# Four groups of a feed-forward's first product begin early, differences of tokens made in it, tokens prepared two products ahead

## The chip, the cores and the metric

The kernel runs on one core of a Trainium2 chip, in one launch. The metric is the device time of one execution in microseconds; lower is better. On a core, TensorE (PE in the profile; its weight loads are PEld) multiplies matrices, VectorE (DVE), ScalarE (ACT) and GpSimd (POOL) work on tiles in SBUF and on the matmuls' results in PSUM, and SyncE (SP) issues most DMAs. Each engine runs its own instructions in the order in which they stand in its queue.

## The reference

One layer of a decoder trunk on 512 tokens of width 1024, in fp32. Three sub-layers follow each other, each between two norms: a mixing layer (a gated unit, block-sparse attention, a convolution), a cross-attention into 256 memory tokens, and a feed-forward of width 4096 with a squared ReLU. The change lies in the last one and in what leads into it:

```python
x = x + rms_norm(memory_cross_attention(h, m, w_xq[l], w_xkv[l], w_xo[l]), post_x_g[l])
h = rms_norm(x, pre_ffn_g[l])
f = jnp.square(jax.nn.relu(h @ w_ff1[l])) @ w_ff2[l]
x = x + rms_norm(f, post_ffn_g[l])
```

## The kernel before, in words

**Splitting.** Every fp32 operand is split into a high and a low part (`split`, lines 113 and 115: ScalarE rounds, VectorE subtracts), and a product takes three matmuls: low by high, high by low, high by high (lines 123 to 125 in `mm3`, line 1067 in the first product).

**Seven products.** Both matmuls of the feed-forward are cut into 2 by 2 blocks and computed with seven block products in place of eight, numbered p 1 to 7, whose operands are sums and differences of blocks. Product 1 uses blocks as they are, products 3 and 5 to 7 need sums or differences on both sides. One block product is 24 matmuls.

**The first product** (`products1`) goes over eight groups of weight columns (`GROUPS`). Four quarters of a group's weights come by SyncE's queue (`Block.load`, line 883) into a ring of `RAWS` buffers. `Block.of` splits a quarter (or a sum) for one product. `Block.sums` makes the weight sums: one addition on VectorE (line 895), a second on VectorE (line 897) or by a DMA that adds (line 868, issued from GpSimd), and a third by such a DMA. Products 1 and 2 of a group need only the first two token tiles; `EARLY` says how many groups have them ahead of the rest in the list of work. `prepare` splits weights `AHEAD` (two) products ahead. `out` takes each product out of PSUM (L1020, L1024, L1025, L1029) and squares it.

**The tokens of the first product.** `project` multiplies the attention's output by `w_xo` for the four token tiles; each tile is then added to x and normalised: squares summed on ScalarE (L189), L178 on VectorE, the power of minus a half on GpSimd (L183), L577 and L204 on VectorE. `put_ff` transposes a tile on TensorE (L935) and splits it; for tiles 2 and 3 it first makes differences and sums (L945, through `s`). Tiles 0 and 1 feed products 1 and 2; all other products need tiles 2 and 3. In the list, tile 2's `put_ff` is called before the second product and tile 3's before the fifth.

**The second product** (`products2`) goes over four chunks of 1024 hidden columns (`NM`). `tokens` makes a product's token operand: sums and differences on VectorE (L1097), then a split. Products 2, 3 and 4 stay in PSUM over all chunks. The others are added into running sums `p_sum`: in chunk 0 copied by ScalarE (L1155); in chunks 1 and 2 products 1 and 5 are copied by ScalarE (L1157) and added by a DMA from GpSimd's queue, and the rest, and all of the last chunk, are added by VectorE (L1159). `prepare` makes tokens and weights one product ahead. In the last chunk the order is 2, 1, 5, 3, 6, 7, 4, and the output's rows are put together as their products end (L1172, L1177), scaled, added and stored (`finish`).

**Order.** A scheduler places the instructions; `ahead(n)` moves an instruction forward in it, and the code's order and the free buffers decide the rest. The loads of the first groups may not be scheduled before the matmul in `ff_after`, which `put_ff` sets at tile 0.

## Time and profile before

| | us |
|---|---|
| median of 3 runs | 734.33 (733.85 to 735.06) |
| profiled execution, device time | 734.33 |
| its span | 732.5 |
| TensorE busy | 695.5 |
| VectorE busy | 530.2 |
| ScalarE busy | 433.0 |
| GpSimd busy | 132.3 |

The span runs from the first instruction to the last; the device time has 1.8 us around it. A matmul's busy time overlaps the next one's, so the distance between two starts tells its pace. An instruction's idle time is that of its engine just before it, and the name behind the arrow is what released it. Names are those of tiles: `small` holds split tokens, sums of tokens and running sums, `quarter` weights, `fhi` and `flo` their high and low parts, `fixed` the rows of x and small columns, `fq` the first product's result.

### The profile page before, as it was taken

To read this page: it belongs to the slowest core of one execution; us is meant where nothing else is said; L and a number is where in the kernel's file an instruction comes from. 1 tells how busy PE (TensorE), PEld (TensorE's weight loads), DVE (VectorE), ACT (ScalarE), POOL (GpSimd) and SP (SyncE) were. 2 spreads that over 40 slices of the span, in tenths; PEclk is the share of its full clock that TensorE was granted. 3 is DMA by queue.
4 is the path that set the end of the run, shared out by engine and by line. 5 is a ranking of instruction groups with operands and counts; after the bars stand their busy time and mean duration, and the time that the engine had idled before them with its cause. 6 is when DMAs were issued, how large, how long until landed. Compare 5 with 4: busy or idle time off the path is not lost.

```text
span 732.5 us, 10699 instructions
## 1 busy us (share of the span) xinstructions
PE 695.5 (95%) x4032; PEld 609.5 (83%) x4032; DVE 530.2 (72%) x803; ACT 433.0 (59%) x776; POOL 132.3 (18%) x143
## 2 busy tenths in 40 slices
PE   8999999997999999999998799999999999999891
PEld 6777888797887889888888799999999888787681
DVE  3479999876774892464469967655666979889797
ACT  5463478797794662353457667666677667375522
POOL 4445343243200110000012010000002021110101
PEclk9999999999999999999999899999999999999997
DMA  8460412143331430011073395567569789695603
GB/s 286 177 230 29 145 40 76 59 158 131 116 114 59 144 115 30 30 57 58 1 223 94 96 221 143 151 168 172 143 179 194 214 186 251 160 247 152 116 0 115
DMA packets 45124, 96.67 MB, mean 132 GB/s; under 512 B 4113, under 2 KB 21265, under 8 KB 45074
## 3 DMA queue, kind: packets, MB, share of 16 engines
q1 hardware_dynamic: 37344, 72.36, 28.9%
q0 software_dynamic: 6336, 23.07, 17.5%
q10 hardware_dynamic: 1394, 0.57, 0.4%
q8 instruction: 31, 0.51, 0.3%
q14 instruction: 19, 0.16, 0.1%
HBM read 70.83 MB, written 2.10 MB: 100 GB/s over the span
## 4 chain that ended last, share of the span: by engine, by line
PE 68%; DVE 17%; ACT 6%; issue 4%; POOL 3%; DMA 2%; DVEq 0%; POOLq 0%; ACTq 0%
PE ps L1067 20%; PE ps L123 15%; PE ps L125 15%; PE ps L124 15%; DVE small L115 2%; DVE flo L115 2%; DVE lo L144 2%; POOL fixed L183 2%; DVE fixed L577 1%; DMA tmp<-in_w_sT 1%; PE ps L685 1%; DVE small L1097 1%; PE ps L697 1%; DVE ps L383 1%; DVE tmp L204 1%
## 5 line engine op out<-in xcount | busy, mean ns | idle before, releaser
L1067 PE MATMUL ps<-small,fhi 128*128 128x256 f32 x896 | 163.8, 285 | 2.7 <-DVE small L115 2.0
L115 DVE TENSOR_TENSOR flo<-quarter,fhi 128x1024 fp32r<-128x1024 f32 x112 | 135.5, 1220 | 38.1 <-ACT fhi L113 34.8
L1067 PEld LDWEIGHTS ps<-small,fhi 128*128 128x128 f32 x896 | 141.2, 194 | 3.8 <-DVE small L115 2.5
L1067 PE MATMUL ps<-small,flo 128*128 128x256 f32 x448 | 127.9, 286 | 3.4 <-DVE flo L115 3.4
L113 ACT ACTIVATE fhi<-quarter 128x1024 fp32r<-128x1024 f32 x112 | 115.3, 1050 | 24.8 <-PE ps L1067 17.2
L123 PE MATMUL ps<-flo,small 128*128 128x512 f32 x224 | 88.2, 394 | 3.3 <-DVE flo L115 2.4
L1067 PEld LDWEIGHTS ps<-small,flo 128*128 128x128 f32 x448 | 86.7, 194 | 4.3 <-DVE flo L115 4.2
L123 PE MATMUL ps<-xl,hi 128*128 128x512 f32 (+1 forms) x256 | 87.3, 341 | 0.5 <-DVE xl L115 0.5
L124 PE MATMUL ps<-fhi,small 128*128 128x512 f32 x224 | 87.7, 392 | 0.0
L125 PE MATMUL ps<-fhi,small 128*128 128x512 f32 x224 | 87.7, 392 | 0.0
L125 PE MATMUL ps<-xh,lo 128*128 128x512 f32 (+1 forms) x256 | 86.3, 337 | 0.4 <-DVE lo L144 0.4
L124 PE MATMUL ps<-xh,hi 128*128 128x512 f32 (+1 forms) x256 | 86.3, 337 | 0.0
L143 ACT ACTIVATE hi<-raw 128x512 fp32r<-128x512 f32 x120 | 70.1, 625 | 14.3 <-PE ps L125 6.8
L868 POOL DMA_DIRECT2D quarter<-quarter x40 | 35.3, 888 | 237.7 <-DVE flo L115 106.5
L144 POOL TENSOR_TENSOR lo<-raw,hi 128x512 fp32r<-128x512 f32 x48 | 63.2, 1331 | 75.7 <-ACT hi L143 66.4
L183 POOL TENSOR_TENSOR fixed<-fixed 128x1 f32<-128x1 f32 x30 | 19.7, 658 | 256.3 <-DVE fixed L178 237.1
L144 DVE TENSOR_TENSOR lo<-raw,hi 128x512 fp32r<-128x512 f32 x72 | 50.6, 732 | 9.7 <-ACT hi L143 9.3
L123 PEld LDWEIGHTS ps<-xl,hi 128*128 128x128 f32 x256 | 48.6, 190 | 5.7 <-issue 0.7
L125 PEld LDWEIGHTS ps<-xh,lo 128*128 128x128 f32 x256 | 48.5, 190 | 5.8 <-DVE lo L144 0.8
L123 PEld LDWEIGHTS ps<-flo,small 128*128 128x128 f32 x224 | 42.3, 189 | 13.2 <-ACT small L113 2.8
L124 PEld LDWEIGHTS ps<-xh,hi 128*128 128x128 f32 x256 | 48.6, 190 | 4.7
L123 PE MATMUL ps<-lo,feat 128*128 128x512 f32 x128 | 50.5, 395 | 0.0
(179 smaller groups left out, 1326.9 us busy)
## 6 DMA issues: line engine op xcount, KB each, us to landing
quarter<-quarter POOLq DMA_DIRECT2D x40, 512.0 KB, 5.2
quarter<-in_w_ff SPq DMA_DIRECT2D x64, 256.0 KB, 4.3
quarter<-in_w_ff SPq DMA_DIRECT2D x32, 512.0 KB, 5.0
raw<-in_w_xk SPq DMA_DIRECT2D x8, 512.0 KB, 3.2
raw<-in_w_xv SPq DMA_DIRECT2D x8, 512.0 KB, 4.2
raw<-in_w_out SPq DMA_DIRECT2D x8, 512.0 KB, 3.5
raw<-in_w_xq SPq DMA_DIRECT2D x8, 512.0 KB, 3.9
raw<-in_w_xo SPq DMA_DIRECT2D x8, 512.0 KB, 4.4
```

The source lines that it names most:

```text
L113: nc.scalar.activation(hi, src, AF.Copy, scale=1.0 if scale is None else scale)
L115: nc.vector.tensor_tensor(out=lo, in0=src, in1=hi.bitcast(F32), op=ALU.subtract)
L123: latest[0] = nc.tensor.matmul(ps, lhsT=lh, rhs=rl, start=start, stop=False)
L124: nc.tensor.matmul(ps, lhsT=lh, rhs=rh, start=False, stop=False)
L125: nc.tensor.matmul(ps, lhsT=ll, rhs=rh, start=False, stop=stop)
L143: nc.scalar.activation(hi, raw[:, c], AF.Copy)
L144: eng.tensor_tensor(out=lo, in0=raw[:, c], in1=hi.bitcast(F32), op=ALU.subtract)
L183: nc.gpsimd.tensor_tensor(out=r, in0=v, in1=neghalf[:, 0:1], op=ALU.pow)
L204: nc.vector.scalar_tensor_tensor(out=xn, in0=src[:, c], scalar=r, in1=g[:, c], op0=ALU.mult, op1=ALU.mult)
L383: nc.vector.scalar_tensor_tensor(out=ac[:, d:], in0=y[:, 0:S - d], scalar=wdw[:, i, CONV - 1 - d:CONV - d], in1=ac[:, d:], op0=ALU.mult, o ...
L868: nc.gpsimd.dma_start(out=out, in_=in_, accum_op=ALU.add)
L1067: nc.tensor.matmul(o, lhsT=w[:, k, c], rhs=x[:, k, :], start=first_, stop=last_, skip_group_check=True)
```

## The change

- `EARLY` goes from 3 to 4 and `RAWS` from 11 to 12: eight block products stand ahead of the rest in the list.
- `ff_after` is set in `project`, once the last blocks of `w_xo` have been asked for, and the first loads and the first two `prepare` calls (now `begin1`) run at tile 0's `put_ff`, so ahead of its transposes and of the other tiles.
- Group 0's sums are asked for one product earlier, and its second sum is made by an adding DMA where it was VectorE.
- For chunk 0 of the second product (`N3S` = 1), two differences of blocks are made in the first product, one into a buffer of its own, one in place.
- In the second product tokens are prepared two products ahead (`AHEAD_X`), weights one ahead as before.
- In the last chunk products 1 and 5 are also copied by ScalarE and added by a DMA.
- The output gain `g5` is loaded in the second product, at its fifth block product.

The diff, without the parts that only rename or move code:

```diff
         wb = [wblock(w[1][b]) for b in range(4)]
+        ff_after[0] = latest[0]
...
-    EARLY = 3
-    RAWS = 11
+    EARLY = 4
+    RAWS = 12
     HALVES = 3
-    g5 = gain(a["post_ffn_g"])
...
-            ff_after[0] = latest[0]
+            begin1()
...
+    N3S = 1
+    n3s = {}
...
+    def begin1():
+        for n in range(EARLY):
+            blocks1[n] = group(n)
+            blocks1[n].load(FIRST, ff_after[0])
+        blocks1[0].load(REST, ff_after[0])
+        for at in range(AHEAD):
+            prepare1(at)
...
+        if (n, p) == (EARLY - 1, 1):
+            blocks1[0].sums(True)
...
-            if (n, p) == (EARLY - 1, 2):
-                blocks[0].sums(False)
...
+            if p == 4 and n % 2 == 1 and n // 2 < N3S:
+                m = n // 2
+                x00, x10, x11 = fq[2 * m][:, :, 0:256], fq[2 * m][:, :, 256:512], fq[2 * m + 1][:, :, 256:512]
+                n3s[m] = feats.tile([P, 4, 256], F32, tag="n3", name=nm("n3"), bufs=max(1, N3S))
+                nc.vector.tensor_tensor(out=n3s[m], in0=x00, in1=x10, op=ALU.subtract)
+                nc.vector.tensor_tensor(out=x10, in0=x10, in1=x11, op=ALU.subtract)
...
+            if m in n3s:
+                sums[m, 1], sums[m, 3] = x(1, 0), n3s[m]
...
-                th, tl = tokens(m, p)
-                ready[at] = (th, tl, [blocks[m][q].of(p) for q in range(2)])
+                ready[at] = [blocks[m][q].of(p) for q in range(2)]
...
+        def prepare_x(at):
+            if at < len(work):
+                ready_x[at] = tokens(*work[at])
...
+        ready_x = {}
+        for at in range(AHEAD_X):
+            prepare_x(at)
         prepare(0)
         for at, (m, p) in enumerate(work):
+            if at == NM:
+                g5.append(gain(a["post_ffn_g"], after=latest[0]))
+            prepare_x(at + AHEAD_X)
             prepare(at + 1)
-            th, tl, ws = ready.pop(at)
+            ws = ready.pop(at)
+            th, tl = ready_x.pop(at)
...
-            part = small([P, 2, 512], F32) if 0 < m < NM - 1 and p in (1, 5) else None
+            part = small([P, 2, 512], F32) if m and p in (1, 5) else None
```

**Behind the token work of the fourth tile.** VectorE's queue, around the end of tile 3's token splits. Before, the last token splits (`small<-xf`), the first product's result (`fq`), then the split of the weight sum of group 0 for product 5 (`quarter_818`), and others:

```order
L115 TENSOR_TENSOR small_799_4027<-xf_804_4032,small_798_4026 128x4x128
L115 TENSOR_TENSOR small_797_4025<-xf_805_4033,small_796_4024 128x4x128
L1020 TENSOR_TENSOR fq_612_3117<-ps_832_4231,tmp_828_4220 128x2x256
L115 TENSOR_TENSOR flo_824_4186<-quarter_818_4127,fhi_823_4185 128x1024
L115 TENSOR_TENSOR flo_830_4223<-quarter_776_3957,fhi_829_4222 128x1024
L895 TENSOR_TENSOR quarter_831_4227<-quarter_778_3963,quarter_825_4189 128x1024
```

After, at the same place:

```order
L115 TENSOR_TENSOR small_796_4027<-xf_804_4035,small_795_4026 128x4x128
L115 TENSOR_TENSOR small_798_4029<-xf_806_4037,small_797_4028 128x4x128
L1030 TENSOR_TENSOR fq_611_3115<-ps_830_4224,tmp_827_4218 128x2x256
L115 TENSOR_TENSOR flo_824_4186<-quarter_758_3856,fhi_823_4185 128x1024
L115 TENSOR_TENSOR flo_829_4221<-quarter_759_3859,fhi_828_4220 128x1024
L115 TENSOR_TENSOR flo_832_4253<-quarter_825_4189,fhi_831_4252 128x1024
```

The three splits are those of group 3's two weights (`quarter_758` and `quarter_759`, products 1 and 2) and of group 0's sum (`quarter_825`): the two added early products' splits stand behind the token work, and the split for product 5 behind them.

**GpSimd's queue at the hand-over.** Before, all norm factors of the tiles (L183) stand together, and the adding DMAs behind them:

```order
L144 TENSOR_TENSOR lo_2217<-raw_2210,hi_2216 128x512
L183 TENSOR_TENSOR fixed<-fixed 128x1 x16
L868 DMA quarter_3957<-quarter_3975 128x1024
L868 DMA quarter_3960<-quarter_3957 128x1024
L868 DMA quarter_3963<-quarter_4189 128x1024
```

After (L190 is the same power, L875 the adding DMA):

```order
L145 TENSOR_TENSOR lo_2217<-raw_2210,hi_2216 128x512
L190 TENSOR_TENSOR fixed<-fixed 128x1 x14
L875 DMA quarter_3862<-quarter_3865 128x1024
L190 TENSOR_TENSOR fixed<-fixed 128x1
L875 DMA quarter_3838<-quarter_3862 128x1024
L190 TENSOR_TENSOR fixed<-fixed 128x1
L875 DMA quarter_3841<-quarter_3838 128x1024
L875 DMA quarter_3844<-quarter_4256 128x1024
```

Group 0's second sum (`quarter_3862`) and third (`quarter_3838`, which reads the second) now stand ahead of the last two factors.

**VectorE's queue in the last chunk.** `small_1002` is the running sum of product 1, `small_1003` that of product 5; `flo_1228` and `flo_1230` are weight splits for product 5. Before:

```order
L115 TENSOR_TENSOR flo_1228_6890<-quarter_1222_6851,fhi_1227_6889 128x1024
L115 TENSOR_TENSOR flo_1230_6894<-quarter_1223_6855,fhi_1229_6893 128x1024
L1159 TENSOR_TENSOR small_1002_5893<-ps_1231_6897,small_1002_5893 128x512
L1159 TENSOR_TENSOR small_1002_5893<-ps_1232_6898,small_1002_5893 128x512
L1177 TENSOR_TENSOR small_1233_6925<-small_1002_5893,ps_996_5887 128x512
L1177 TENSOR_TENSOR small_1233_6925<-small_1002_5893,ps_997_5888 128x512
L570 TENSOR_TENSOR tmp_1235_6929<-small_1233_6925,gain_609_3113 128x512
L570 TENSOR_TENSOR tmp_1237_6934<-small_1233_6925,gain_609_3113 128x512
L1097 TENSOR_TENSOR small_1238_6936<-small_1224_6883,fq_616_3121 128x1024
L1159 TENSOR_TENSOR small_1003_5894<-ps_1246_6952,small_1003_5894 128x512
L1097 TENSOR_TENSOR small_1239_6938<-fq_617_3122,small_1238_6936 128x1024
L1159 TENSOR_TENSOR small_1003_5894<-ps_1247_6953,small_1003_5894 128x512
```

After, where L1206 is an output row, L577 its scaling, and L1114 a token sum:

```order
L115 TENSOR_TENSOR flo_1233_6901<-quarter_1225_6860,fhi_1232_6900 128x1024
L115 TENSOR_TENSOR flo_1245_6950<-quarter_1177_6616,fhi_1244_6949 128x1024
L115 TENSOR_TENSOR flo_1247_6954<-quarter_1178_6618,fhi_1246_6953 128x1024
L1206 TENSOR_TENSOR small_1237_6934<-small_1002_5894,ps_996_5888 128x512
L1206 TENSOR_TENSOR small_1237_6934<-small_1002_5894,ps_997_5889 128x512
L577 TENSOR_TENSOR tmp_1239_6938<-small_1237_6934,gain_1062_6112 128x512
L577 TENSOR_TENSOR tmp_1241_6943<-small_1237_6934,gain_1062_6112 128x512
L115 TENSOR_TENSOR small_1243_6946<-small_1226_6888,small_1242_6945 128x1024
L1114 TENSOR_TENSOR small_1251_6987<-fq_615_3119 128x1024
L115 TENSOR_TENSOR flo_1255_6994<-quarter_1171_6604,fhi_1254_6993 128x1024
L115 TENSOR_TENSOR flo_1257_6999<-quarter_1172_6606,fhi_1256_6998 128x1024
```

The two additions into `small_1002` are gone, as are those into `small_1003`. The splits for product 3 (`flo_1245`, `flo_1247`) stand ahead of the first output row, which reads `small_1002`; the token split for product 6 (`small_1243`) and its weight splits (`flo_1255`, `flo_1257`) stand behind it.

## Rows read from the trace of the kernel before

**Rows 1.** Part 1 of the page: busy microseconds, share of the span and instruction count of each engine.
```profile
PE 695.5 (95%) x4032; PEld 609.5 (83%) x4032; DVE 530.2 (72%) x803; ACT 433.0 (59%) x776; POOL 132.3 (18%) x143
```

**Rows 2.** Stretches of the span: microseconds from its start and length, then for each engine its busy time and its instructions, TensorE's granted clock as a share of full speed, the busy share of the DMA engines and what they moved.
```profile
409.00:412.00 3.00, 1.01 (x4) 0.59 (x4) 3.00 (x6) 2.15 (x4) 0.00 (x0) 0.87 0.00 0
412.00:415.00 3.00, 1.32 (x6) 1.32 (x7) 3.00 (x4) 2.21 (x3) 0.00 (x0) 0.50 0.00 0
415.00:418.00 3.00, 3.00 (x16) 3.00 (x16) 3.00 (x3) 0.00 (x0) 0.00 (x0) 0.50 0.52 158
...
415.00:560.00 145.00, 145.00 (x1195) 144.63 (x1194) 95.02 (x90) 95.17 (x128) 14.94 (x17) 0.99 0.68 170
...
690.00:700.00 10.00, 7.56 (x27) 5.73 (x26) 10.00 (x11) 4.66 (x5) 0.00 (x0) 0.83 0.07 14
```

**Rows 3.** TensorE in order of time from 376 to 422 us: start, duration, engine, line, operation, tiles, count, and in brackets its idle time before, with what ended it.
```profile
380.46 1.04 PE L935 MATMUL ps<-fixed,tmp 128*128 128x128 f32 x8
...
386.21 0.50 PE L1067 MATMUL ps<-small,fhi 128*128 128x256 f32 x2 [0.62 <-ACT fhi L113]
...
399.46 0.38 PE L1067 MATMUL ps<-small,flo 128*128 128x256 f32 x1 [0.53 <-DVE flo L115]
...
410.15 1.10 PE L1067 MATMUL ps<-small,fhi 128*128 128x256 f32 x4 [1.96 <-DVE small L115]
413.68 0.58 PE L1067 MATMUL ps<-small,flo 128*128 128x256 f32 x1 [2.43 <-DVE flo L115]
...
418.22 0.40 PE L1067 MATMUL ps<-small,flo 128*128 128x256 f32 x2
```

**Rows 4.** Who waited for whom in SyncE's queue from 345 to 420 us: total, times, longest.
```profile
SPq L883 <- DVE fixed L577: 39.3, 1, 39.3
```

**Rows 5.** ScalarE in order of time, from 360 to 400 us.
```profile
372.96 0.60 ACT L189 ACTIVATE tmp<-ps 128x512 f32<-128x512 f32 x1 [1.67 <-PE ps L125]
...
385.11 2.00 ACT L113 ACTIVATE fhi<-quarter 128x1024 fp32r<-128x1024 f32 x2
```

**Rows 6.** GpSimd in order of time, from 380 to 400 us. L183 is the power of minus a half that turns a mean square into the norm's factor; L868 issues an adding DMA.
```profile
384.85 1.39 POOL L183 TENSOR_TENSOR fixed<-fixed 128x1 f32<-128x1 f32 x1 [2.92 <-DVE fixed L178]
389.09 0.55 POOL L183 TENSOR_TENSOR fixed<-fixed 128x1 f32<-128x1 f32 x1 [2.85 <-DVE fixed L178]
392.49 1.40 POOL L183 TENSOR_TENSOR fixed<-fixed 128x1 f32<-128x1 f32 x1 [2.85 <-DVE fixed L178]
397.08 1.06 POOL L868 DMA_DIRECT2D quarter<-quarter  x1 [3.19 <-DVE xf L945]
```

**Rows 7.** VectorE in order of time, from 376 to 418 us.
```profile
377.77 1.42 DVE L204 SCALAR_TENSOR_TENSOR tmp<-fixed,gain_row 128x512 f32<-128x512 f32 x2 [0.73 <-POOL fixed L183]
...
392.27 1.22 DVE L115 TENSOR_TENSOR flo<-quarter,fhi 128x1024 fp32r<-128x1024 f32 x1
393.92 1.42 DVE L204 SCALAR_TENSOR_TENSOR tmp<-fixed,gain_row 128x512 f32<-128x512 f32 x2 [0.44 <-POOL fixed L183]
395.26 1.22 DVE L897 TENSOR_TENSOR quarter<-quarter,quarter 128x1024 f32<-128x1024 f32 x1
396.39 0.69 DVE L945 TENSOR_TENSOR xf<-ps,tmp 128x512 f32<-128x512 f32 x1
...
412.42 2.35 DVE L115 TENSOR_TENSOR flo<-quarter,fhi 128x1024 fp32r<-128x1024 f32 x2
```

**Rows 8.** TensorE in order of time in the second product, from 624 to 720 us.
```profile
625.23 0.50 PE L123 MATMUL ps<-flo,small 128*128 128x512 f32 x1 [0.43 <-DVE small L1159]
...
664.03 0.50 PE L123 MATMUL ps<-flo,small 128*128 128x512 f32 x1 [0.43 <-DVE small L1159]
...
693.96 0.47 PE L123 MATMUL ps<-flo,small 128*128 128x512 f32 x1 [2.44 <-DVE flo L115]
...
695.31 0.63 PE L125 MATMUL ps<-fhi,small 128*128 128x512 f32 x1
...
716.98 0.39 PE L124 MATMUL ps<-fhi,small 128*128 128x512 f32 x1
717.21 0.39 PE L125 MATMUL ps<-fhi,small 128*128 128x512 f32 x1
```

**Rows 9.** VectorE in order of time at the end, from 676 us on.
```profile
686.13 0.69 DVE L1159 TENSOR_TENSOR small<-ps,small 128x512 f32<-128x512 f32 x1 [0.67 <-PE ps L125]
...
712.19 0.69 DVE L1159 TENSOR_TENSOR small<-ps,small 128x512 f32<-128x512 f32 x1 [0.37 <-PE ps L125]
...
726.58 2.74 DVE L577 SCALAR_TENSOR_TENSOR fixed<-tmp,fixed 128x512 f32<-128x512 f32 x4 [0.50 <-POOL fixed L183]
```

**Rows 10.** GpSimd in order of time in the second product, from 600 us on.
```profile
677.80 0.87 POOL L868 DMA_DIRECT2D quarter<-quarter  x1 [4.89 <-DVE flo L115]
678.93 0.89 POOL L868 DMA_DIRECT2D quarter<-quarter  x1 [0.27 <-issue]
...
686.79 0.87 POOL L868 DMA_DIRECT2D quarter<-quarter  x1 [2.56 <-DMA quarter<-quarter]
```

**Rows 11.** Issue to landing of adding DMAs: first the one issued at 678.93; then the minimum, median and maximum over all of them (L868); then the same over the four that add a product into its running sum.
```profile
quarter<-quarter POOLq DMA_DIRECT2D x1, 512.0 KB, 7.5
...
DMA to landing us min/median/max: 4.5/5.2/9.8
...
DMA to landing us min/median/max: 5.3/8.4/9.8
```

More of the change, by code (lines that the diff above doesn't have):

```diff
@@ L120, in trunk @@
     latest = [None]
+    ff_after = [None]
     def mm3(ps, lh, ll, rh, rl, start, stop):
@@ L168, in trunk, with not_before, gain @@
     nc.gpsimd.memset(neghalf, -0.5)
-    def gain(src, queue=nc.sync):
+    def not_before(d, other):
+        if other is not None:
+            tc.add_manual_dep(d.ins, other.ins.name, mybir.DependencyInfo(
+                mybir.DependencyClass.NoSync, mybir.DependencyReason.DATA), reason="room")
+    def gain(src, queue=nc.sync, after=None):
         g = gains.tile([P, D], F32, tag="gain", name=nm("gain"))
-        queue.dma_start(out=g, in_=bass.AP(tensor=src.tensor, offset=src.offset, ap=[[0, P], [1, D]]))
+        not_before(queue.dma_start(out=g, in_=bass.AP(tensor=src.tensor, offset=src.offset, ap=[[0, P], [1, D]])),
+                   after)
         return g
@@ L876, in __init__, with load @@
             self.raw = {}
-        def load(self, ats, not_before=None):
+        def load(self, ats, after=None):
             for at in ats:
@@ L974, in group @@
         return Block([P, 4, 256], src)
-    def products1(xs):
-        work = [(n, p) for n in range(EARLY) for p in (1, 2)]
-        for n in range(GROUPS):
-            one = [(n, p) for p in ((5, 6, 3, 7) if n < EARLY else (1, 5, 2, 6, 3, 7))]
-            work += one[:1] + ([(n - 1, 4)] if n else []) + one[1:]
-        work.append((GROUPS - 1, 4))
-        blocks = {}
-        ready = {}
+    N3S = 1
+    n3s = {}
+    work1 = [(n, p) for n in range(EARLY) for p in (1, 2)]
+    for n in range(GROUPS):
+        one = [(n, p) for p in ((5, 6, 3, 7) if n < EARLY else (1, 5, 2, 6, 3, 7))]
+        work1 += one[:1] + ([(n - 1, 4)] if n else []) + one[1:]
@@ new lines, in trunk, with prepare1 @@
+    work1.append((GROUPS - 1, 4))
+    blocks1 = {}
+    ready1 = {}
+    FIRST, REST = ((0, 0), (1, 0)), ((0, 1), (1, 1))
+    def begin1():
[5 more added lines that the diff above has]
+            prepare1(at)
+    def prepare1(at):
+        if at >= len(work1):
+            return
+        n, p = work1[at]
+        ready1[at] = blocks1[n].of(p)
+        if p == 1 and n >= EARLY:
+            blocks1[n].sums(False)
+        if (n, p) == (EARLY - 1, 1):
+            blocks1[0].sums(True)
+        if p == 6 and n + 1 < EARLY:
+            blocks1[n + 1].sums(False)
+        if p == 5 and n + 1 < GROUPS:
+            if n + 1 >= EARLY:
+                blocks1[n + 1] = group(n + 1)
+                blocks1[n + 1].load(FIRST)
+            blocks1[n + 1].load(REST)
@@ L984, in products1 @@
+    def products1(xs):
+        work, ready = work1, ready1
         banks = {}
         kept = {}
-        FIRST, REST = ((0, 0), (1, 0)), ((0, 1), (1, 1))
-        for n in range(EARLY):
-            blocks[n] = group(n)
-            blocks[n].load(FIRST, ff_after[0])
-        blocks[0].load(REST, ff_after[0])
-        def prepare(at):
-            if at >= len(work):
-                return
-            n, p = work[at]
-            ready[at] = blocks[n].of(p)
-            if p == 1 and n >= EARLY:
-                blocks[n].sums(False)
-            if (n, p) == (EARLY - 1, 2):
-                blocks[0].sums(False)
-            if p == 6 and n + 1 < EARLY:
-                blocks[n + 1].sums(False)
-            if p == 5 and n + 1 < GROUPS:
-                if n + 1 >= EARLY:
-                    blocks[n + 1] = group(n + 1)
-                    blocks[n + 1].load(FIRST)
-                blocks[n + 1].load(REST)
@@ L1045, in out @@
                     square(quarter(1, 0), two(ps))
-        for at in range(AHEAD):
-            prepare(at)
         for at, (n, p) in enumerate(work):
```

12 lines of the change are left out of this document (5 added, 7 removed).

## The prediction

> **What bounds the kernel now.** I read the busy shares first: TensorE is busy 95% of the span, so only its gaps, its clock and the tail behind its last product can be won [rows 1]. The table by stretch came next: the clock is full nearly everywhere and half in two places, both in the feed-forward; between 415 and 560 us TensorE has no gap at all, with VectorE busy 95.02 of 145 us there [rows 2]. Then TensorE in order of time: in the hand-over from the cross-attention's output projection to the first feed-forward product it has short waits (0.62 and 0.53 us among them) and two long ones, 1.96 us for a token split and 2.43 us for a weight's low part; behind the second the matmuls run at half clock until 418.2, at some 0.21 us apart in place of 0.12, which costs about 4.5 × (1 − 0.12 / 0.21) = 1.9 us [rows 2, 3]. In the second product there are two waits of 0.43 us for VectorE's additions into the running sums, and one of 2.44 us at 693.96, again followed by half clock [rows 8]. Last, the tail: after the last matmul only VectorE, GpSimd and the store work [rows 9].
>
> Three stretches can change: the hand-over, the two small waits, and the last chunk with its tail.
>
> **The hand-over.** What ends the long waits? VectorE. From 393.92 it runs without a gap: the last tile's two norm products, then one 1.22 us sum, three 1.22 us splits and 21 operations on 128x512 until the weight split at 412.42, whose first instruction lets TensorE go on at 413.68 [rows 3, 7]. The starts at 395.26 and 396.39 give a pitch of 1.13 us to a big operation; (412.42 − 395.26 − 4 × 1.13) / 21 = 0.60 to a small one.
>
> The new order has the same 21 small operations there, two splits and no sum (that one became a DMA), so 2 × 1.13 + 21 × 0.60 = 14.9 us in place of 17.2: 2.3 us less. It is not all won, for two reasons.
> - The earlier loads. Before, the first of them waits 39.3 us for the first tile's norm [rows 4]; now they start some 7 us sooner, and three weight roundings come onto ScalarE ahead of the second tile's square sum. Three take 3 × 1.0 = 3.0 us; ScalarE was idle 1.67 us there, so the square sum is 1.3 us later [rows 5]. On VectorE a weight split of 1.13 stands ahead of that tile's norm. Its norm products, ready at 379.2 (377.77 + 1.42), come at about 381.6, and the transposes that ran at 380.46 without a wait now wait [rows 3, 7]: 1.1 us for TensorE, and for the last two tiles behind it.
> - GpSimd's queue. Two of group 0's sums are DMA additions that now stand ahead of the fourth tile's two roots (L183), one ahead of each; the second waits until the first has landed. The first goes out behind the root that ran at 384.85 for 1.39, now 1.1 later, so at 387.4 (its weights have landed by then); with the 5.2 us of a middling addition [rows 11] it lands at 392.6; the second's issue takes 1.06 [rows 6], and the last root, due at 392.49 + 1.1 = 393.6, starts at 393.7 to 394.0: 0.4 us late at most.
>
> So the last norm is 1.5 us late, the chain 2.3 us shorter: the split that frees TensorE is 0.8 us earlier. TensorE has two more matmuls done by then (0.2 us). I take −1.0. The wait itself stays, for the splits of the two extra products stand behind all token operations of the fourth tile, and no other work is put into the gap; so the clock falls again. Bounds: −2.5 (no delay), and +3.3 if the first addition lands after 9.8 us, the longest in rows 11 (397.2, then 1.06: the root 4.7 us late). The row of 5.2 is nearer: the 9.8 was of a sum with another addition right ahead of it.
>
> There is one row against this. The root took 1.40 us at 392.49 beside a 1.22 us VectorE operation and 0.55 us at 389.09 without one [rows 6, 7]. The Trainium skill (SBUF — State Buffer, "SBUF: two separate sides") says that GpSimd and VectorE share a port pair under an exclusive lock, and that descriptors of a DMA issued from GpSimd starve behind VectorE. By it both new issues would be held by some 0.85 us each (1.40 − 0.55) in this dense stretch, and the gain of 1.0 falls to nothing; the row on the root agrees with the rule, while the issue at 397.08 took 1.06 beside VectorE's work, against 0.87 at 677.80. I keep the row of the issue.
>
> **The middle.** The two differences moved into the first product cost 2 × 1.13 us of VectorE where it has 50 us to spare [rows 2]: nothing. Preparing tokens two products ahead takes token work from in front of VectorE's additions into the sums, and these are what ended the two waits of 0.43 us: −0.9. The gain vector's load, moved among the weight loads, is wanted only in the last chunk: nothing. Bounds: 0 if another row holds these additions, −0.9 otherwise.
>
> **The last chunk and the tail.** Call E1 the end of its product 1 (686.1 [rows 9]); the span ends 46.4 us later. Today VectorE adds that product into its sum as soon as it ends. Now ScalarE copies it (two copies) and GpSimd adds it by a DMA that stands behind the last weight sum, issued at E1 + 0.7 [rows 10]; it is issued at about E1 + 1.7. Of two additions 1.1 us apart (677.80 and 678.93) the second landed after 7.5 us, and the four sums of this kind took 5.3 to 9.8 [rows 10, 11]. With 7.5 the sum is there at S = E1 + 9 (a little under, 8.8, as no weight loads run beside it).
>
> What waits for S? VectorE's first output row, and it stands in VectorE's queue ahead of the tokens and weight splits of product 6 (p 6), the one after product 3. Product 3's wait of 2.44 us goes, and its half clock (0.43 us a matmul from 694.5 to 697.9: some 1.7 us), since its tokens and splits now stand ahead of that row [rows 8]; it ends at E1 + 10.9 (two products of 24 matmuls, 0.227 us from start to start [rows 8]). But p 6 starts at S + 4 × 0.60 + 3 × 1.13 = S + 5.8 = E1 + 14.6, 3.7 us after TensorE is free, and at half clock for as long as before. p 6 then ends at S + 5.8 + 5.4 + 1.9, p 7 at S + 18.5. From p 7's end to the span's end is 20.35 us today (712.15, where the addition at 712.19 begins [rows 9], to 732.5). Now two sums of 2.35 us together are out of the first rows' way, one split of 1.13 comes in front of the last product's second half, which then waits some 4 us for it, at half clock; I count 19.6. Together S + 38.1 = E1 + 46.9, against E1 + 46.4: +0.5. Bounds, by the landing alone: 5.3 with an issue at E1 + 1.2 gives S = E1 + 6.5 and −1.8; 9.8 behind an issue at E1 + 1.7 gives S = E1 + 11.5 and +3.2. Four additions of 0.60 fewer on VectorE change nothing while it waits for S.
>
> The Trainium skill (DMA: Bandwidth & Descriptors, "Anatomy of one DMA — SWDGE (gpsimd) path") fits such a DMA by 2.0 us and its bytes at 436 GB/s, an estimate of 3.2 us for 512 KB; by it p 6 would not be held at all, the last chunk would gain about 5 us and the sum would be near −7. Of all additions of this trace none landed in under 4.5 us [rows 11], so the measurement decides.
>
> **Sum.** −1.0 − 0.9 + 0.5 = −1.4 us. The profiled execution took 734.33 us (span 732.5), which is also the median shown, so 732.9 us.
>
> **Rivals.**
> - The sum lands at the quick end. For it: in the last chunk no weight loads run. Against: another addition is in flight. End −1.8, total −3.7: 730.6.
> - The sum lands before p 6 wants anything, by S = E1 + 5.1: no wait, no half clock, p 7 ends at E1 + 21.8 and the span at E1 + 41.4, so −5.0 at the end: 727.4. Against it: the shortest landing, 4.5, behind the issue at E1 + 1.2 still gives E1 + 5.7. The Trainium skill's page DMA: Bandwidth & Descriptors (the section above) speaks for it.
> - The two extra products do fill the gap. For it: their weights are in early, and the rounding of both is on ScalarE in time. Against: VectorE's order. It would win 1.96 + 2.43, and the 1.9 of half clock, with the middle and the end as above: 727.6.
> - Slower: the sum of p 1 lands late and holds VectorE's queue. Place: VectorE's first output row of the last chunk. It decides from a landing of about 8.5 us (where the end costs more than the rest wins); at 9.8 the end is +3.2, and if the DMA additions ahead of the roots eat the hand-over's gain as well, −0.9 + 3.2 = +2.3: 736.6.
> - The change doesn't do what it says: the early groups stand behind the tokens, and the 0.43 us waits were held by something else, with the end neutral: 734.2.
>
> **How the numbers follow.** Chances: forecast 0.45 (its own range 731.4 to 734.4), quick landing 0.16, no hold 0.04, gap filled 0.06, late landing 0.20, no effect 0.09. Faster by over 0.2% (1.47 us, about what a measurement of this kernel can tell) is half of the forecast (0.22) with the next three: 0.48. Slower is the late landing, 0.20; the rest, 0.32, is within 0.2%. The range 729.5 to 736.6 leaves out the filled gap and the case without a hold, and the outer parts of the two landings.
>
> **What would show it.** TensorE's first long wait of the hand-over, now for a low part with four early groups: if it ends near 412.8 the first term is right; if there is no wait of over 1 us between 400 and 420, the filled gap is. A wait of GpSimd for an addition's landing ahead of the fourth tile's last root would show its queue. No waits of 0.43 us before 670. In the last chunk: VectorE idle for several microseconds before its first output row, released by an addition's landing, and TensorE idle ahead of p 6 by about 3.7 us; no such wait, and the end is better than I say. A second wait, of some 4 us, in the last product. I am wrong if the clock stays full through the hand-over, or if the time between the first and the second product, where I expect nothing, moves.

## The result, and the profile after

The changed kernel took 739.84 us (median of 6, 738.05 to 742.95) against 733.73 us before: ratio 1.0089, 95% interval 1.0062 to 1.0115. It is slower by 0.9%; the forecast was 732.9 us. The profiled execution is the quickest of the six (738.05 us, span 736.3).

Part 1 of the page after answers to [rows 1]: TensorE is as busy as before, in a longer span.

```profile
PE 697.7 (95%) x4032; PEld 610.1 (83%) x4032; DVE 527.8 (72%) x798; ACT 435.6 (59%) x780; POOL 134.7 (18%) x146
```

TensorE in order of time after, its waits from 396 us on (columns as in [rows 3]; L1075 is the first product's matmul, L124 and L126 those of the second):

```profile
400.64 0.47 PE L1075 MATMUL ps<-small,fhi 128*128 128x256 f32 x2 [2.03 <-DVE xf L948]
...
408.16 0.50 PE L1075 MATMUL ps<-small,fhi 128*128 128x256 f32 x2 [1.31 <-ACT fhi L113]
...
411.30 0.58 PE L1075 MATMUL ps<-small,flo 128*128 128x256 f32 x1 [1.69 <-DVE flo L115]
...
433.64 0.47 PE L1075 MATMUL ps<-small,fhi 128*128 128x256 f32 x2 [0.47 <-DVE fq L1030]
...
443.02 0.38 PE L1075 MATMUL ps<-small,flo 128*128 128x256 f32 x1 [0.27 <-DVE flo L115]
...
458.94 0.39 PE L1075 MATMUL ps<-small,flo 128*128 128x256 f32 x1 [1.26 <-DVE flo L115]
...
557.70 0.47 PE L124 MATMUL ps<-flo,small 128*128 128x512 f32 x1 [0.60 <-DVE flo L115]
...
628.55 0.50 PE L124 MATMUL ps<-flo,small 128*128 128x512 f32 x1 [2.41 <-DVE small L1188]
...
667.49 0.50 PE L124 MATMUL ps<-flo,small 128*128 128x512 f32 x1 [0.57 <-DVE small L1188]
...
703.15 0.80 PE L124 MATMUL ps<-flo,small 128*128 128x512 f32 x1 [2.73 <-DVE flo L115]
...
723.15 0.50 PE L124 MATMUL ps<-flo,small 128*128 128x512 f32 x1 [4.58 <-DVE flo L115]
```

Read against [rows 3] and [rows 8]: in place of the two long waits of the hand-over (1.96 and 2.43) stand 2.03, 1.31, 1.69 and one of 0.45 us at 409.11 that isn't shown. Three waits between 430 and 460 and one at the start of the second product (0.60) are new. The two waits of 0.43 in the second product have become 2.41 and 0.57. The 2.44 of [rows 8] is gone, and 2.73 and 4.58 stand in the last chunk.

To compare stretches I count from t0, the start of the first tile's transposes in the hand-over (374.13 before, 372.50 after). Executions differ by about 2 us ahead of it: the 1000th matmul starts at 200.4 before and at 198.7, 198.4 and 200.7 in three profiles of the changed kernel, long before its first new load (350 us). In both kernels the transposes start 0.24 or 0.23 us behind the start of the matmul in front of them, so t0 is the same point of the work in both. The table by stretch (columns as in [rows 2]; the number behind PE's busy time is its instructions), from t0 + 11.8 to t0 + 60 and from there to t0 + 90, of the kernel before:

```profile
385.93:434.13 48.20, 41.98 (x318) 40.32 (x319) 42.05 (x52) 32.56 (x52) 7.20 (x9) 0.93 0.52 120
434.13:464.13 30.00, 30.00 (x252) 30.00 (x251) 19.60 (x19) 19.86 (x27) 2.29 (x3) 1.00 0.71 186
```

and of the changed kernel:

```profile
384.30:432.50 48.20, 42.33 (x325) 41.12 (x325) 38.15 (x51) 30.07 (x50) 7.13 (x8) 0.93 0.44 99
432.50:462.50 30.00, 28.00 (x229) 27.42 (x228) 21.20 (x21) 17.80 (x26) 3.47 (x4) 1.00 0.79 194
```

At 0.12 us a matmul, the hand-over has won (325 − 318) × 0.12 = 0.8 us, and the 30 us behind it lose (252 − 229) × 0.12 = 2.8 us. From t0 to the end of the last chunk's product 1 (E1) it took 686.1 − 374.1 = 312.0 us before and 689.6 − 372.5 = 317.1 after; from E1 to the end of the span 46.4 and 46.7. So the whole loss lies ahead of the last chunk: −0.8, +2.8, +0.6 at the start of the second product, and 2.41 + 0.57 − 2 × 0.43 = +2.1 in it make 4.7 of the 5.1 us.

This profile is of the quickest execution, and one cost is missing from it. Here the clock stays full behind the wait of 2.41 us; in the second and third profile of the same kernel (runs `again` and `again2` below) it falls to half there (0.50 from 631 to 633 us in `again`, so 1.2 of 2.4 GHz). The first 4 us behind that wait, in this profile and in that of `again`:

```profile
628.55:632.55 4.00, 4.00 (x18) 3.31 (x19) 4.00 (x5) 0.36 (x1) 0.79 (x1) 1.00 0.76 262
```

```profile
629.49:633.49 4.00, 4.00 (x11) 3.18 (x12) 4.00 (x5) 0.36 (x1) 0.79 (x1) 0.62 0.74 262
```

The 168 matmuls of that chunk take 38.8 us before, 40.8 in this profile and 42.4 in the two others: where the clock falls, the wait costs 3.6 us and not 2.0.

What stands behind the waits? VectorE after, in order of time (columns as in [rows 7]; L901 and L899 are weight sums, L1206 an output row):

```profile
393.81 1.42 DVE L211 SCALAR_TENSOR_TENSOR tmp<-fixed,gain_row 128x512 f32<-128x512 f32 x2 [1.94 <-POOL fixed L190]
...
410.02 4.62 DVE L115 TENSOR_TENSOR flo<-quarter,fhi 128x1024 fp32r<-128x1024 f32 x4
...
440.61 1.22 DVE L901 TENSOR_TENSOR quarter<-quarter,quarter 128x1024 f32<-128x1024 f32 x1 [2.32 <-DMA quarter<-in_w_ff]
...
456.53 1.23 DVE L901 TENSOR_TENSOR quarter<-quarter,quarter 128x1024 f32<-128x1024 f32 x1 [2.53 <-DMA quarter<-in_w_ff]
...
697.20 1.29 DVE L1206 TENSOR_TENSOR small<-small,ps 128x512 f32<-128x512 f32 x2 [3.68 <-DMA small<-small]
```

The split that frees TensorE starts at 410.02 (first of four) and not at 412.42 [rows 7]. But two weight sums, at 440.61 and 456.53, wait 2.32 and 2.53 us for weights to land, and TensorE waits (0.27 and 1.26) for the split right behind each. The first of the two new differences stands between them, at 442.88. Such a wait of a sum alone is not new: before, one waited longer, and TensorE had no gap.

```profile
436.04 1.23 DVE L895 TENSOR_TENSOR quarter<-quarter,quarter 128x1024 f32<-128x1024 f32 x1 [3.43 <-DMA quarter<-in_w_ff]
```

Further on in the changed kernel, the first output row waits 3.68 us for a DMA addition. ScalarE after, with a token rounding (L113) and the copies of product 1 in the last chunk (L1186):

```profile
622.16 1.06 ACT L113 ACTIVATE small<-fq 128x1024 fp32r<-128x1024 f32 x1 [2.49 <-DMA small<-small]
...
688.22 0.60 ACT L1186 ACTIVATE small<-ps 128x512 f32<-128x512 f32 x1 [3.26 <-PE ps L126]
689.58 0.60 ACT L1186 ACTIVATE small<-ps 128x512 f32<-128x512 f32 x1 [0.76 <-PE ps L126]
```

The rounding at 622.16 waits 2.49 us for the landing of an addition into a running sum, although its operand is a block of `fq`. The addition still in flight is that of product 5's copy, issued at 616.30. Everything on VectorE behind the rounding is late, down to the addition into the sum that ends TensorE's wait of 2.41. GpSimd after (L190 the tiles' factor, L875 an adding DMA), answering to [rows 6] and [rows 10]:

```profile
385.48 1.39 POOL L190 TENSOR_TENSOR fixed<-fixed 128x1 f32<-128x1 f32 x1 [2.91 <-DVE fixed L185]
387.07 1.06 POOL L875 DMA_DIRECT2D quarter<-quarter  x1 [0.20 <-issue]
388.60 0.56 POOL L190 TENSOR_TENSOR fixed<-fixed 128x1 f32<-128x1 f32 x1 [0.47 <-DVE fixed L185]
392.29 0.89 POOL L875 DMA_DIRECT2D quarter<-quarter  x1 [3.13 <-DVE fixed L185]
392.91 0.86 POOL L190 TENSOR_TENSOR fixed<-fixed 128x1 f32<-128x1 f32 x1
...
616.30 0.88 POOL L875 DMA_DIRECT2D small<-small  x1 [8.93 <-ACT small L1186]
...
690.06 0.86 POOL L875 DMA_DIRECT2D quarter<-quarter  x1 [2.59 <-DMA quarter<-quarter]
690.67 1.16 POOL L875 DMA_DIRECT2D small<-small  x1
```

### The profile page after: what moved, and what is told of

Its sections match the earlier page's. It is cut to its first block, busy times and chain, and to the rows that moved or that the text cites. A ratio compares the mean times of both kernels' runs of the same rounds, so it can differ in the third digit from the quotient of the medians.

```text
span 736.3 us, 10717 instructions
## 1 busy us (share of the span) xinstructions
PE 697.7 (95%) x4032; PEld 610.1 (83%) x4032; DVE 527.8 (72%) x798; ACT 435.6 (59%) x780; POOL 134.7 (18%) x146
## 5 line engine op out<-in xcount | busy, mean ns | idle before, releaser
L1075 PE MATMUL ps<-small,fhi 128*128 128x256 f32 x896 | 164.1, 286 | 4.6 <-DVE xf L948 2.0
L1075 PEld LDWEIGHTS ps<-small,fhi 128*128 128x128 f32 x896 | 141.4, 194 | 5.9 <-ACT fhi L113 5.0
L113 ACT ACTIVATE fhi<-quarter 128x1024 fp32r<-128x1024 f32 x112 | 115.7, 1050 | 31.0 <-PE ps L1075 21.4
L1075 PE MATMUL ps<-small,flo 128*128 128x256 f32 x448 | 128.0, 286 | 3.2 <-DVE flo L115 3.2
L124 PE MATMUL ps<-flo,small 128*128 128x512 f32 x224 | 89.0, 397 | 10.9 <-DVE flo L115 7.9
L1075 PEld LDWEIGHTS ps<-small,flo 128*128 128x128 f32 x448 | 86.9, 194 | 4.0 <-DVE flo L115 4.0
L126 PE MATMUL ps<-fhi,small 128*128 128x512 f32 x224 | 88.4, 395 | 0.0
L124 PE MATMUL ps<-xl,hi 128*128 128x512 f32 (+1 forms) x256 | 87.3, 341 | 0.5 <-DVE xl L115 0.5
L126 PE MATMUL ps<-xh,lo 128*128 128x512 f32 (+1 forms) x256 | 86.2, 337 | 0.0
L875 POOL DMA_DIRECT2D quarter<-quarter x41 | 35.8, 873 | 244.5 <-DVE flo L115 107.1
L144 ACT ACTIVATE hi<-raw 128x512 fp32r<-128x512 f32 x120 | 70.1, 625 | 16.8 <-PE ps L126 10.0
L190 POOL TENSOR_TENSOR fixed<-fixed 128x1 f32<-128x1 f32 x30 | 20.0, 667 | 242.8 <-DVE fixed L185 223.5
L124 PEld LDWEIGHTS ps<-flo,small 128*128 128x128 f32 x224 | 42.9, 191 | 21.6 <-DVE flo L115 8.1
L124 PEld LDWEIGHTS ps<-xl,hi 128*128 128x128 f32 x256 | 48.6, 190 | 5.7 <-issue 0.7
L126 PEld LDWEIGHTS ps<-xh,lo 128*128 128x128 f32 x256 | 48.5, 190 | 5.1
L124 PE MATMUL ps<-lo,feat 128*128 128x512 f32 x128 | 50.6, 395 | 0.0
```

The source lines that it names most:

```text
L113: nc.scalar.activation(hi, src, AF.Copy, scale=1.0 if scale is None else scale)
L124: latest[0] = nc.tensor.matmul(ps, lhsT=lh, rhs=rl, start=start, stop=False)
L126: nc.tensor.matmul(ps, lhsT=ll, rhs=rh, start=False, stop=stop)
L144: nc.scalar.activation(hi, raw[:, c], AF.Copy)
L190: nc.gpsimd.tensor_tensor(out=r, in0=v, in1=neghalf[:, 0:1], op=ALU.pow)
L875: nc.gpsimd.dma_start(out=out, in_=in_, accum_op=ALU.add)
```

## The experiments

Every run is compared with the kernel before on the same chip; the ratios have 95% intervals. All start from the changed kernel.

**The base again** (`again`, unchanged).

> The changed kernel once more, as the base of this call. Expected: 736 to 741 us, 0.5 to 1.1% slower than before; TensorE's waits as in its first trace: about 2.0 us in all between 430 and 460 us, 2.4 near 628, 0.6 near 667, 2.7 near 703 and 4.6 near 723.

739.95 us, 1.007 (1.0047 to 1.0092), with 0.60, 2.07 and 1.22 between 430 and 460, and 2.38, 0.57, 2.61 and 4.57 later. The waits are the change's, not one execution's; their sizes between 430 and 460 vary with the landings: the sum that waited 2.32 us in the first profile waits 4.10 here, and TensorE's wait behind it is 2.07 in place of 0.27.

**The last chunk by VectorE** (`lastdve`).

```diff
-            part = small([P, 2, 512], F32) if m and p in (1, 5) else None
+            part = small([P, 2, 512], F32) if 0 < m < NM - 1 and p in (1, 5) else None
```

> The changed kernel with products 1 and 5 of the last chunk added by VectorE, as before. Theory (the landing of product 1's sum holds VectorE's queue for 3.68 us, and with it product 6): the wait near 703 goes, VectorE gets four additions of 0.60 back, and from the end of product 1 to the end of the span it takes 42 to 44 us in place of 46.75: 3 to 4 us faster than the changed kernel. Rival (the tail is VectorE's own work, the hold is only moved): within 0.7 us of the changed kernel.

736.53 us, 1.0034 (1.0014 to 1.0055): 3.4 us faster than the base. TensorE's long waits from 630 us on:

```profile
632.36 0.50 PE L124 MATMUL ps<-flo,small 128*128 128x512 f32 x1 [2.35 <-DVE small L1188]
...
701.00 0.50 PE L124 MATMUL ps<-flo,small 128*128 128x512 f32 x1 [0.61 <-DVE flo L115]
...
724.56 0.79 PE L124 MATMUL ps<-flo,small 128*128 128x512 f32 x1 [4.20 <-DVE flo L115]
```

The hold in front of product 6 is 0.61 where it was 2.61. From E1 to the end it took 738.1 − 695.0 = 43.1 us. So tokens two ahead are worth 46.4 − 43.1 = 3.3 us in the last chunk, and the DMA addition takes back 46.7 − 43.1 = 3.6: the change put both in, and the end stood still.

**Tokens one ahead, last chunk by VectorE** (`x1lastdve`: the edit above and `AHEAD_X = 1`).

> As the run before it, and tokens one product ahead. Theory (two products ahead is what makes the additions late): the wait of 2.41 near 628 is back to 0.4 and the 0.57 near 667 too, so the end of product 1 of the last chunk comes 2.1 us earlier; but product 3's splits stand late again and its 2.44 us wait with half clock returns, +3 to +4: in sum 1 to 2 us slower than the run before it. Rival (the wait near 628 comes from elsewhere): the 2.41 stays.

741.68 us, 1.0089 (1.0062 to 1.0116), 5 us slower than the run before it (single times of both spread over 5 to 7 us), where I expected 1 to 2. The last chunk behaved (2.43 near 701 is back, 46.3 us from E1). But the wait near 628 did not go; it became 1.60 at 617.54, 0.48 at 618.73 and 1.40 at 632.44. Two ahead is therefore not the cause by itself. VectorE in this run:

```profile
613.78 1.23 DVE L1114 TENSOR_TENSOR small<-small,fq 128x1024 f32<-128x1024 f32 x1 [3.60 <-DMA small<-small]
```

Now a token sum (L1114), not a rounding, waits 3.60 us for an addition's landing. What both share is the pool of 14 buffers called `small`: operands, token sums, the copies `part` that a DMA reads, and the running sums all turn in it.

**Three early groups** (`early3`: `EARLY = 3`, `RAWS = 11`).

> The changed kernel with three early groups and eleven weight buffers, as before. Theory (with four groups early, twelve buffers leave the later groups' loads too late): the waits of 0.47, 0.27 and 1.26 between 430 and 460 go, the gap of the hand-over grows by 0.6 to 1 us: 1 to 1.5 us faster than the changed kernel at the end of the first product. Rival (these waits come from the two differences made in the first product): they stay, and the time does not move or gets longer.

736.44 us, 1.0033 (1.0013 to 1.0053), 3.5 us faster than the base, more than expected. The same two stretches from its t0 (373.88):

```profile
385.68:433.88 48.20, 43.54 (x331) 42.56 (x331) 40.56 (x52) 32.36 (x54) 8.88 (x10) 0.93 0.61 145
433.88:463.88 30.00, 30.00 (x252) 30.00 (x251) 21.45 (x20) 20.28 (x28) 1.75 (x2) 1.00 0.66 171
```

331 and 252: no wait between 430 and 460, so the fourth group (with its twelfth buffer) is what brought those waits. The 13 matmuls more than before in the hand-over are not a gain, for here t0 itself is late. With three groups weight roundings on ScalarE and a weight split on VectorE stand ahead of the first tile's norm, and TensorE waits for that norm:

```profile
373.88 1.32 PE L938 MATMUL ps<-fixed,tmp 128*128 128x128 f32 x8 [0.80 <-DVE tmp L211]
```

These transposes start 1.18 us behind the start of the matmul in front of them (372.70), where it was 0.24 us before and 0.23 with four groups. From that matmul to the last one of the first product it took 186.2 us before (373.89 to 560.12), 189.2 in the changed kernel and 186.1 with three groups (372.70 to 558.75). The early loads, with group 0's DMA sum, win nothing on balance; without the fourth group they lose nothing either.

**One more small buffer** (`early3_s15`: three groups, `bufs=15` for `small`).

> Three early groups and eleven weight buffers, and 15 buffers for the tiles called small in place of 14. Theory (the ring of these buffers: a token split made two products ahead takes the buffer of a product that a DMA is still adding, ScalarE waits 2.47 us for its landing at 619.67, and VectorE's additions behind it come late): the 2.40 us wait of TensorE near 626 falls to 0.5 or less, 2 us faster than with three early groups alone (736.4). Rival (VectorE's order alone: token splits stand ahead of the additions): the wait stays at 2 us or more.

736.79 us, 1.0036 (1.0022 to 1.0051); 2.43 near 628 and ScalarE's 2.50 for the landing are as they were, where I expected them to go. One more buffer shifts who takes which, and the rounding still waits for the addition of product 5's copy (issued at 616.05), so the run does not decide between the buffer and VectorE's order.

**Both undone** (`early3_lastdve`).

> Three early groups and eleven buffers, and the last chunk's products 1 and 5 added by VectorE. If the two costs are separate, as I take it, their gains add: 3.5 and 3.4 off the changed kernel, so 733 us, level with before. Rival (one covers the other): 735 or more.

734.12 us, 0.9986 (0.9971 to 1.0002). The two gains add (739.95 − 3.5 − 3.4 = 733.0) to within 1.1 us.

**Only the earlier loads, group 0's DMA sum and the gain's late load** (`x1lastdve_e3n0`: three groups, one ahead, `N3S = 0`, last chunk by VectorE).

> Of the change only the earlier loads, the DMA addition for group 0's sum and the late load of the output gain: three early groups, tokens one product ahead, no differences in the first product, the last chunk by VectorE. Theory: the first product ends 1.4 us earlier than before (as with three early groups), and the second product is as before, with waits of 0.4, 0.4 and 2.4: 732.5 to 733. This also tells where the 1.60 us wait near 617 came from that tokens one ahead showed with the differences made early: theory, two token sums fewer shift the ring of small buffers, so without them it goes; rival (the gain's load or the order of weights and tokens): it stays.

734.06 us, 1.0004 (0.9990 to 1.0018), where I expected 732.5 to 733. The 1.60 near 617 is gone, with waits of 0.66, 0.86 and 2.43 against 0.43, 0.43 and 2.44 before. From t0 to the end its profile is 1.7 us shorter than before (356.7 and 358.3), but t0 is 0.95 late here too; from the matmul ahead of it to the first product's last it took 186.3 us against 186.2. So the earlier loads and group 0's DMA sum together are worth about nothing.

**Thirteen weight buffers** (`raws13n0`: four groups, `RAWS = 13`, `N3S = 0`).

> Four early groups with 13 weight buffers, and no differences in the first product (their buffer makes the room). Theory (the ring of weight buffers is what makes the loads of the next groups late): the waits between 430 and 460 us, 2.0 to 3.9 in sum, fall under 0.5, and the first product ends 1.5 to 3 us earlier than in the changed kernel. Rival (the order of the four groups on VectorE and GpSimd): they stay.

739.58 us, 1.0072 (1.0057 to 1.0087), against 1.0070 for `again`: no gain. Only one wait (0.34) is left between 430 and 460, but the hand-over had 319 matmuls in its 48 us where the base's profiles had 325 and 329. The waits behaved, the time did not. The run `n0` below differs from this one in the thirteenth buffer alone and had 0.93 us of waits there, so most of what went, went with the differences. SyncE's loads wait for buffers in every version; the longest such wait between 380 and 470 us is 29.1 us in the changed kernel, 29.2 in `n0`, 16.8 with thirteen buffers and 20.8 before.

**The copies in a buffer of their own** (`e3_ld_part`: three groups, last chunk by VectorE).

```diff
-            part = small([P, 2, 512], F32) if m and p in (1, 5) else None
+            part = feats.tile([P, 2, 512], F32, tag="part", name=nm("part"), bufs=1) if 0 < m < NM - 1 and p in (1, 5) else None
```

> Three early groups, the last chunk by VectorE, and the copies of products 1 and 5 (of chunks 1 and 2) in a buffer of their own and no longer among those called small. Theory (the tokens for the next chunk's product 1, made two products ahead, take the buffer of product 5's copy, which is free only when its addition has landed): ScalarE's wait of 2.5 us for the landing near 620 goes and TensorE's 2.4 us near 626 falls to 0.7 or less: 731.5 to 732.5, 1.5 to 2.5 us below the run with three early groups and the last chunk by VectorE (734.1). Rival (VectorE's order alone): the landing's wait goes, TensorE's stays at 1.5 or more.

731.40 us, 0.9965 (0.9949 to 0.9981): 2.7 us under the same kernel without it (734.12, measured at another time beside its own runs of the kernel before; by the means it is 2.0, give or take 1.2), and faster than both kernels of this document. ScalarE's rounding, VectorE's additions into the sum, and TensorE's waits from 600 us on:

```profile
619.14 1.06 ACT L113 ACTIVATE small<-fq 128x1024 fp32r<-128x1024 f32 x1 [2.00 <-PE ps L125]
```

```profile
623.65 0.68 DVE L1188 TENSOR_TENSOR small<-ps,small 128x512 f32<-128x512 f32 x1
624.81 0.69 DVE L1188 TENSOR_TENSOR small<-ps,small 128x512 f32<-128x512 f32 x1 [0.48 <-PE ps L126]
```

```profile
658.46 0.50 PE L124 MATMUL ps<-flo,small 128*128 128x512 f32 x1 [1.02 <-DVE flo L115]
...
692.00 0.50 PE L124 MATMUL ps<-flo,small 128*128 128x512 f32 x1 [0.61 <-DVE flo L115]
...
715.58 0.80 PE L124 MATMUL ps<-flo,small 128*128 128x512 f32 x1 [4.20 <-DVE flo L115]
```

No wait for a landing, the second addition now waits for TensorE (0.48), and the 2.4 us is gone; VectorE's queue still has a token split and two weight splits right ahead of the additions. So the buffer was the cause. That chunk takes 38.1 us here, against 42.4 in the profile of the same kernel without the own buffer, where the clock fell behind the wait.

**The same without the two differences** (`e3_ld_part_n0`: also `N3S = 0`).

> The same without the two differences made in the first product. Theory: these moved 2.4 us of VectorE's work out of the second product's first chunk, where nothing waits for it; no wait goes or comes: within 0.7 us of the run before it. Rival: without them a wait of over 0.5 us appears where the second product starts.

730.63 us, 0.9962 (0.9943 to 0.9981): no difference that shows. With three groups the two differences are worth nothing that can be measured here.

**Group 0's second sum by VectorE** (`e3_ld_part_sd`: `blocks1[0].sums(False)`).

> As the first of this call, and group 0's second sum by VectorE as before. Theory (GpSimd's second issue, which waits for the first addition to land, makes the fourth tile's last root 1.1 us late: VectorE idle 1.94 us before it in the changed kernel): the root comes 1.1 us earlier, the sum's 1.13 us of VectorE comes back behind it, so the split that frees TensorE moves by less than 0.3 us and the time stays within 0.7 us. Rival (the landing costs the hand-over more than the sum did): 1 us faster.

733.89 us, 0.9996 (0.9983 to 1.0010): 2.5 us slower than `e3_ld_part`, neither theory's. VectorE in the hand-over, in this run and then the same norm products in `e3_ld_part`:

```profile
390.88 1.22 DVE L901 TENSOR_TENSOR quarter<-quarter,quarter 128x1024 f32<-128x1024 f32 x1
392.02 0.21 DVE L185 TENSOR_SCALAR fixed<-fixed 128x1 f32<-128x1 f32 x1
...
394.49 1.42 DVE L584 SCALAR_TENSOR_TENSOR fixed<-tmp,fixed 128x512 f32<-128x512 f32 x2 [0.53 <-POOL fixed L190]
...
399.66 1.42 DVE L211 SCALAR_TENSOR_TENSOR tmp<-fixed,gain_row 128x512 f32<-128x512 f32 x2 [0.79 <-POOL fixed L190]
```

```profile
396.08 1.42 DVE L211 SCALAR_TENSOR_TENSOR tmp<-fixed,gain_row 128x512 f32<-128x512 f32 x2 [1.97 <-POOL fixed L190]
```

The sum (L901, 390.88) stands ahead of the fourth tile's first step (L185, 392.02), and that tile's norm products come at 399.66, 24.2 us behind its t0 (375.50), against 396.08 − 375.08 = 21.0 in `e3_ld_part`. Once the loads are early, the DMA addition is worth 2.5 us; it makes up for what they cost.

**Four groups in this version** (`e4_ld_part_n0`: `EARLY = 4`, `RAWS = 12`).

> The version without differences in the first product, with the copies' own buffer and the last chunk by VectorE, but with the change's four early groups and twelve weight buffers. Theory (the fourth group costs by itself, through weights that land late between 430 and 460 us): 3 to 3.5 us slower than with three groups (730.6), so 733.5 to 734.2, with waits of 2 us or more in sum between 430 and 460. Rival (the cost came from the two differences or from the other parts): 731.5 or less, no such waits.

731.48 us, 0.9966 (0.9952 to 0.9980), where I expected 733.5 or more. Waits of 0.62 and 0.53 between 430 and 460, against 2.0 to 3.9 in sum in the base's three profiles. So the rival held: the fourth group costs much less here than with the differences.

**The change without the differences** (`n0`, beside the base, `again2`).

> The changed kernel without the two differences in the first product, all else as changed. Theory A (four groups cost much only together with the differences: weight sums that land late leave VectorE no slack, and the differences take 2.4 us of it): the waits between 430 and 460 us fall to about 1.2 in sum, as in the version with the own buffer, and it is 2 to 3 us faster than the changed kernel. Theory B (four groups cost by themselves): within 1 us of the changed kernel, waits of 2 us or more.

> The changed kernel again, as the base beside it: 739 to 740.5 us.

740.27 us, 1.0083 (1.0061 to 1.0104), beside 742.16, 1.0104 (1.0082 to 1.0127). TensorE's waits between 430 and 460 without the differences:

```profile
435.04 0.48 PE L1075 MATMUL ps<-small,fhi 128*128 128x256 f32 x2 [0.47 <-DVE fq L1030]
...
444.60 0.39 PE L1075 MATMUL ps<-small,flo 128*128 128x256 f32 x1 [0.46 <-DVE flo L115]
```

0.93 in sum against 0.45 + 1.82 + 1.23 = 3.5 in `again2`. The last of the three is gone, as the second weight sum starts 14.1 us behind the first here and 15.9 us in `again2`, where a difference stands between them. The medians lie 1.9 apart, just under what theory A gave; the two intervals overlap, but of the twelve times only one of `n0` (741.77) reaches those of the base (741.71 and up). Theory A holds by the waits, and about in size.

## Why the prediction was wrong, by its own steps

Two terms failed: the zero for everything between the hand-over and the second product, and the −0.9 for the middle, which had the wrong sign. The hand-over and the last chunk came out as forecast.

- **The hand-over, −1.0: right.** The split that frees TensorE came 0.8 us earlier from t0 (37.5 against 38.3; forecast 0.8), the wait stayed and the clock fell. Its parts came out too: the last norm products 1.5 us later (21.3 against 19.8; forecast 1.5), the chain behind them 2.3 us shorter (16.2 against 18.5; forecast 2.3). One part was lucky: the last root, whose input was there at about 391.9, ran at 392.91, 0.9 us late by GpSimd's queue in place of 0.4 at most, but took 0.86 us in place of 1.40. The first loads came 20 us sooner (350.0 in place of 369.9) and not some 7; with three groups their roundings and splits therefore also hold the first tile's norm, and on balance the earlier loads are worth nothing there.
- **Behind the hand-over: the step that failed first.** I read in [rows 2] that TensorE has no gap from 415 to 560 and VectorE 50 us to spare, and priced the fourth group and the two differences there at nothing. An average over 145 us doesn't show how little time the splits had to spare behind a sum that waits for its weights. With four groups such sums wait 2.32 and 2.53 us (rows above), a difference stands between them, and TensorE lost 2.8 us. Without the fourth group this loss is gone (252 matmuls). Without the differences most of the waits are gone (0.93 us in place of 3.5), but not most of the time: from the matmul ahead of t0 to the first product's last it took 186.1 to 186.8 us in the six profiles with three groups and the DMA sum, 188.0 to 189.2 in the three with four groups and no differences, and 188.4 to 190.8 in the five with both. By the averages (186.4, 188.6 and 189.9) the fourth group costs about 2.2 us by itself and the differences 1.3 more, the latter from ranges that overlap. That it's the weight buffers that delay the loads stays argued; with a thirteenth the longest wait for a buffer fell from 29.2 to 16.8 us, but the time did not follow.
- **The middle, −0.9: wrong in sign, +2.1 by the waits, and 1.6 more where the clock fell behind the long one.** I took tokens two ahead to clear VectorE's way to the additions. I didn't ask which buffer the early token takes. It takes that of product 5's copy, free only when its addition has landed. With an own buffer for the copies the wait for the landing and TensorE's 2.4 us behind it went, and the time fell by some 2 to 2.7 us: shown. Such a wait doesn't need tokens two ahead: with tokens one ahead and the differences, a token sum met one too (3.60 us).
- **The last chunk and tail, +0.5: right in its mechanism, +0.35, and in size with some luck.** The landing was at E1 + 7.6 (forecast 8.8), the hold 2.73 (3.7), product 6 began 5.95 behind the landing (5.8), the wait in the last product was 4.58 (some 4). From product 6's start to the end it took 33.2 us where the forecast's terms give 32.3, so two misses of about 1 us cancel. The Trainium skill's fit (DMA: Bandwidth & Descriptors, "Anatomy of one DMA — SWDGE (gpsimd) path"), an estimate of 3.2 us for 512 KB, would have had it there before TensorE waits; the trace disagrees: from 690.67, where this addition is issued, to VectorE's start at 697.20 are 6.5 us.
- **The rivals.** None was it. The gap was not filled, the early splits did stand behind the tokens. The late landing was the slower rival I priced, and it is not what made the kernel slower. The root took 1.39 us at 385.48, beside a VectorE operation with two operands in SBUF, and 0.56 at 388.60; the last one took 0.86 at 392.91, with VectorE idle. The DMA issue at 387.07 took 1.06 us and that at 392.29 took 0.89, so the 0.85 per issue that I priced did not come. The Trainium skill's port rule (SBUF — State Buffer, "SBUF: two separate sides") agrees with the first two roots and doesn't explain the third; it ties the starving of descriptors to VectorE operations in a 2-port performance mode, a condition that the prediction left out.

## What to carry to other kernels

Work that is moved ahead holds a buffer longer, and the next tile to take that buffer inherits its wait: for each tile made earlier, name the buffer that it takes and who must let it go, a DMA's landing above all. Price an addition in a stretch with spare engine time by the time its inputs have to spare, not by the busy share. When several edits go together, take them apart even where the sum is near nothing: here one part was worth 3.3 us and another took it back, and three groups with an own buffer for the copies and the last chunk by VectorE made a version that is 0.35% faster than before. And check that the point from which stretches are counted does not itself move with the edit.

## What was not expected of the hardware

An adding DMA of 512 KB with only one other addition beside it, and no weight loads, still took 6.5 us from issue to its reader's start; in the trace before the additions into sums took 5.3 to 9.8 [rows 11]. And executions of one kernel differ by 2 us and more (738.05 to 742.95 for the changed one), partly ahead of the change's first instruction: t0 was 372.50, 372.16 and 374.47 in three profiles of the same kernel. Part of it comes later: behind the same wait of 2.4 us the clock stayed full in three profiles of versions that have it and fell to half in six, 1.6 us apart. What decides between the two is not shown.

Open: how much of the fourth group's cost reaches the end. Two pairs that differ in it gave 3.5 us (with the differences) and 0.9 (without them and with the own buffer), the second with intervals that overlap; in the profiles of the second pair the first product is 2.8 us longer with four groups, and most of that comes back in the second product, for a reason that I did not look for.
